# A hybrid decoder block on one core: the attention branch in seven block products, the pooling on GpSimd

## The chip, the cores and the metric

The kernel runs on one core of a Trainium2 chip. The core has TensorE (PE, matmuls; its weight loads are PEld), VectorE (DVE), ScalarE (ACT), GpSimd (POOL) and SyncE (SP, which issues DMAs); each takes its own instructions in order. The metric is the device time of one launch in microseconds (us); less is better.

## What is computed

The input x is 1024 tokens by 1024 channels, in float32. The part of the reference that the change touches:

```
xn = rmsnorm(x); u, q, k, v, gates = split(xn @ w_in + b_in)     # u: 512 wide, gates: 2 x 1024
for gi, w in enumerate((2, 4, 8, 16)):                           # four groups of 128 channels of u
    c  = cumsum(u_group over time)
    pooled = (c[t] - c[t - w]) / min(t + 1, w)                   # mean of the last w tokens
    diff[gi] = pooled - u_group
yp = einsum(diff, w_pool) * pool_scale                           # pooling branch, 512 wide
ya = sliding_window_attention(q, k, v, sinks)                    # attention branch, 512 wide
y  = sigmoid(gate0) * (yp @ w_branch_pool) + sigmoid(gate1) * (ya @ w_branch_attn)
x  = x + rmsnorm(y @ w_out)
x  = x + rmsnorm(relu(rmsnorm(x) @ w_up) ** 2 @ w_dn)
```

## The kernel before

Everything is feature-major: a tile holds 128 features in its partitions and 1024 tokens. Each float32 operand is split into two parts, hi (a rounded copy, made by ScalarE) and lo (the rest, a difference made by VectorE; both in `split`, L101 and L104), and each product is three matmul passes: hi·hi, hi·lo, lo·hi. A matmul is 128×128 weights by 512 tokens.

**Seven products for a pair of tiles.** The gate, u, out, up and down products are done for two output tiles (a pair p) and two halves of the tokens at a time, in seven products of block sums in place of eight of blocks (class `Pairs`, line 482 on). The operands of the moving side are the blocks B11, B22, B21 and the sums T1 to T4 (`OPERAND`); VectorE makes the sums of the weights of a pair (L530, L531, L535, L536), ScalarE and VectorE split them, and the seven results are summed in PSUM or by VectorE.

**The gate loop** (L1085 to L1120) runs over p = 1 to 6. A round holds five products of TensorE, 12 matmuls each: 6 of pair p, 4 and 3 of pair p−1, 5 and 7 of pair p. ScalarE copies banks out. VectorE adds product 5 into the result of pair p−1 (L1095, it reads the PSUM bank `e`; product 3 of pair p−1 goes into the same bank behind it), makes the weight sums of pair p+1, splits them, adds the third product (L1110, from PSUM) and multiplies both tiles by the norm's factor (L1105, L1112, `rb`). The gates' sigmoid follows on ScalarE and the result is stored.

**The pooling** lies in the same loop. Pairs 8 and 9 are the four tiles of u. `gate_finish` (L798) multiplies such a tile by `rb`; `chain_start` (L753) adds the bias on ScalarE and stores u to DRAM; `chain_steps` (L760) doubles a window on VectorE: t[s] = f[s] + f[s − step], an add of 128×1024 (L770) and a small copy of its first columns (L771). The four groups (windows 4, 16, 2, 8 started in p = 1, 2, 3, 4) take ten such adds in all, in p = 3 to 6 and one behind the loop. Later, while the attention product runs, u is loaded again (`pool_load`), VectorE scales and subtracts (`pool_diff`, L784 to L786) and the result is split (`pool_split`).

**The attention product** (L1146 to L1215) is done without block sums: eight output tiles m, each with 4 × 2 × 3 matmuls (`mm_fm`, L461). Its operand is four tiles of ya, split into `yahi` and `yalo` (L1055, L1060), the weights are split tile by tile (`ba_split`), and VectorE multiplies each result by its gate (`ba_mul`). The pooling branch's product follows with the same function, operand `yp`.

**Load 19** is the raw weight tile of u's last quarter; pair 9 takes it. SP issues it at the start of the gate product, behind the last stores of the attention; the sums of pair 9 (L530 at 172 us) need it. Loads of the normalised input's raw tiles `xr` follow on SP (`load_x`, L825). GpSimd issues DMAs that add into DRAM or SBUF (L438, L968) and is otherwise idle from the attention to the end.

All engines' instructions in these parts stand in the order in which the code is written (`manual_schedule`); DMAs of SP and POOL stand in their engine's order too.

Of the kernel before, what the change touches and what calls it, by code (L numbers as in the profile page):

```python
# [8 lines left out]
F32 = mybir.dt.float32  # L9
# [41 lines left out]
def block_kernel(ctx: ExitStack, tc, xt, x, consts, vecs, sinks, b_qkv, g_post, g_mlp, g_mlp_post,  # L51
# [16 lines left out]
    def nm(s):  # L68
        cnt[0] += 1
        return f"{s}_{cnt[0]}"  # L70
# [22 lines left out]
    def flat(t):  # L93
        return t.rearrange("p a b -> p (a b)")
# [657 lines left out]

    def chain_start(gi):  # L753

        f = chains[gi][0]
        act.activation(f, f, AF.Identity, bias=vec[:, V_BU + gi:V_BU + gi + 1])
        nc.sync.dma_start(u_dram[gi], f)
        chains[gi] = f, 1

    def chain_steps(gis):  # L760

        for gi in gis:
            f, step = chains[gi]
            if gi % 2 == 0:
                t = g32([S])
            elif 2 * step < WINDOWS[gi]:
                t = ga_.tile([P, S], F32, tag="ga", name=nm("t"))
            else:
                t = gate_result()
            dve.tensor_tensor(t[:, step:], f[:, step:], f[:, :S - step], ALU.add)  # L770
            dve.tensor_copy(t[:, :step], f[:, :step])  # L771
            chains[gi] = t, 2 * step

    pool_raw = {}

    def pool_load(gi):

        u = pool_raw[gi] = yy.tile([P, S], F32, tag="y", name=nm("d"))
        nc.sync.dma_start(u, u_dram[gi])

    def pool_diff(gi):

        w, (src, step), u = WINDOWS[gi], chains.pop(gi), pool_raw[gi]
        dve.scalar_tensor_tensor(u[:, w - 1:], src[:, w - 1:], 1.0 / w, u[:, w - 1:], ALU.mult, ALU.subtract)  # L784
        dve.tensor_tensor(src[:, :w - 1], src[:, :w - 1], cst[:, C_CNT:C_CNT + w - 1], ALU.mult)
        dve.tensor_tensor(u[:, :w - 1], src[:, :w - 1], u[:, :w - 1], ALU.subtract)  # L786

    def pool_split(gi):

        ysp[gi] = [flat(yp_tile([2, 512])) for _ in range(2)]  # L790
        split(*ysp[gi], pool_raw.pop(gi))
# [22 lines left out]
    def gate_result():  # L814
        return flat(yy.tile([P, 2, 512], F32, tag="y", name=nm("z")))
# [36 lines left out]
    with tc.manual_schedule(engines={mybir.EngineType.PE, mybir.EngineType.DVE, mybir.EngineType.Activation}):  # L852
# [99 lines left out]
    def g32(shape):  # L952
        return gp.tile([P] + shape, F32, tag="g", name=nm("g"))
# [23 lines left out]
    with tc.manual_schedule(engines={mybir.EngineType.PE, mybir.EngineType.DVE, mybir.EngineType.Activation,  # L977
                                     mybir.EngineType.SP}):
        gt.load(19, g32([NK, P]))
# [8 lines left out]
        for p in (6, 7):  # L988
            gt.m2(p)
            nc.sync.dma_start(f_spill(p), gt.f0.pop(p))  # L990
            if p == 6:
                gt.split37(9, ar)
                scale_gate(1)
# [52 lines left out]
    asp = [[None, None], [None, None]]  # L1046
    attn_raw = {}

    def attn_load(th, kh):
        t = attn_raw[th, kh] = xp.tile([P, 2, 512], F32R, tag="x", name=nm("yalo"))  # L1050
        nc.sync.dma_start(f32(t), y_dram[2 * kh:2 * kh + 2, :, th * 512:(th + 1) * 512].rearrange("m p q -> p m q"))

    def attn_hi(th, kh):
        hi, lo = xp.tile([P, 2, 512], F32R, tag="x", name=nm("yahi")), attn_raw[th, kh]
        act.copy(hi, f32(lo))  # L1055
        asp[th][kh] = (hi, lo)

    def attn_lo(th, kh):
        hi, lo = asp[th][kh]
        dve.tensor_tensor(lo, f32(lo), f32(hi), ALU.subtract)  # L1060

    ORDER = ((0, 0), (1, 0), (0, 1), (1, 1))

    STARTS, STEPS = {1: 1, 2: 3, 3: 0, 4: 2}, {3: (1, 1), 4: (0, 3), 5: (3, 3, 3), 6: (2, 2)}
# [4 lines left out]
    with tc.manual_schedule(engines=MANUAL):  # L1069
# [14 lines left out]
        gate_finish(17, f1s.pop(8))  # L1084
        for p in range(1, 7):  # L1085
# [5 lines left out]
            chain_steps(STEPS.get(p, ()))  # L1091
# [3 lines left out]
            dve.tensor_tensor(f1[:, V], f1[:, V], e, ALU.add)  # L1095
# [23 lines left out]
            if p in (2, 3):  # L1119
                early_third(p + 6)  # L1120

# [5 lines left out]
    def yp_tile(shape):  # L1127
        return xp.tile([P] + shape, F32R, tag="x", name=nm("yp"))

    za, ba_raw, ba_gate, ba_w, ba_bs = [], {}, {}, {}, {}  # L1130

    def ba_load(m):
        ba_gate[m] = gate_load(8 + m)
        ba_raw[m] = stage([4, P])
        nc.sync.dma_start(ba_raw[m], w_ba[m])

    def ba_split(m):
        ba_w[m] = wslot([4, P]), wslot([4, P])
        split(*ba_w[m], ba_raw.pop(m))

    def ba_mul(m):
        z = ba_gate.pop(m)
        for th, b in enumerate(ba_bs.pop(m)):
            sl = slice(th * 512, (th + 1) * 512)
            dve.tensor_tensor(z[:, sl], z[:, sl], b, ALU.mult)
        za.append(z)  # L1146

    with tc.manual_schedule(engines=MANUAL):
# [4 lines left out]
        chain_steps((2,))  # L1153
# [5 lines left out]
        attn_hi(*ORDER[0])  # L1159
        attn_lo(*ORDER[0])  # L1160
        act.copy(f1[:, U], c)
        gt.mm(e, 6, 3, after=True)
        dve.tensor_tensor(f1, f1, rb, ALU.mult)
        gate_sigmoid(13, f1)
        b7, b5 = bank("mm"), bank("at")
        gt.mm(b7, 7, 7)
        dve.tensor_tensor(f0[:, V], f0[:, V], e, ALU.add)
        ba_load(0)
        ba_load(1)
        ba_split(0)  # L1170
        attn_hi(*ORDER[1])
        dve.tensor_tensor(f0, f0, rb, ALU.mult)
        gate_sigmoid(12, f0)
        attn_hi(*ORDER[2])
        gt.mm(b5, 7, 5)
        dve.tensor_tensor(g1[:, V], u2, b7, ALU.add)
        attn_lo(*ORDER[1])
        gt.mm(b7, 7, 4, after=True)
        dve.tensor_tensor(g1[:, V], g1[:, V], b5, ALU.add)
        attn_lo(*ORDER[2])  # L1180
        attn_hi(*ORDER[3])
        ba_split(1)
        attn_lo(*ORDER[3])
        gt.mm(b5, 7, 3, after=True)
        dve.tensor_tensor(g1[:, U], u2, b7, ALU.add)
        dve.tensor_tensor(g1, g1, rb, ALU.mult)
        gate_sigmoid(15, g1)
        ba_load(2)
        POOLS = (1, 0, 3, 2)
        pool_load(POOLS[0])  # L1190
        pool_load(POOLS[1])
        for m in range(8):
            if m < 5:
                ba_load(m + 3)
            ba_bs[m] = bank("mm"), bank("mm")
            mm_fm(ba_bs[m], *ba_w[m], lambda k, hl, th: asp[th][k // 2][hl][:, k % 2, :], 4)
            if m:
                ba_mul(m - 1)
            else:
                dve.tensor_tensor(u2, u2, b5, ALU.add)  # L1200
                dve.tensor_tensor(g0, g0, rb, ALU.mult)
            if m < 6:
                ba_split(m + 2)
            if m == 0:
                gate_sigmoid(14, g0)
            if 1 < m < 6:
                pool_split(POOLS[m - 2])
            if 0 < m < 5:
                pool_diff(POOLS[m - 1])
            if 0 < m < 3:  # L1210
                pool_load(POOLS[m + 1])
# [68 lines left out]
    def bp_split(m):  # L1280
        w_of[m] = wslot([4, P]), wslot([4, P])
        split(*w_of[m], wraw_of.pop(m))
# [10 lines left out]
    with tc.manual_schedule(engines=MANUAL):  # L1293
        q1 = [wo_raw("B11", c, wraw) for c in range(2)]
        for c in range(2):
            wo_add(q1[c], "B12", c)
# [4 lines left out]
        for m in range(8):  # L1301
# [6 lines left out]
            if m:  # L1308
                bp_mul(m - 1)
            else:  # L1310
                ba_mul(7)
            if m < 7:
                bp_split(m + 1)
            if m:
                merged(m - 1)
            if m in (4, 5):
                b11[m - 4] = wo_raw("B11", m - 4, stage)
# [733 lines left out]
```

## Time and profile before

| | |
|---|---|
| median of 3 runs | 1103.01 us (1102.08 to 1103.38) |
| the profiled execution | 1100.77 us |
| its span, first to last instruction | 1098.8 us |
| granted TensorE clock | 0.998 |
| PE, DVE, ACT, POOL busy | 1088.6, 794.8, 593.8, 75.2 us |
| last attention heads and start of the gate product | 160 to 213 us |
| gate loop | 213 to 292 us |
| last gate pair | 292 to 311 us |
| attention product, then pooling product | 311 to 354, 354 to 398 us |

The table's first time is that of the launch; the profile belongs to one execution, and its span leaves out 1100.77 − 1098.8 = 2.0 us around the instructions. In rows of the trace a time of start stands first and a duration second, both in us; a bracket at the end gives the idle time of the engine ahead of the instruction and what ended it. A row of a group gives busy time and the mean in ns. A row of a DMA issue stands at the engine that issues it (SPq is SP's).

### The profile page before, as it was taken

What the parts mean: (1) busy time and instruction counts of PE and PEld (TensorE: products, weight loads), DVE (VectorE), ACT (ScalarE), POOL (GpSimd) and SP (SyncE); (2) the same over time, 40 slices, a digit from 0 to 9 for tenths busy, and PEclk for the clock granted to TensorE, in tenths of its full rate; (3) what the DMA queues carried; (4) which work ended last, traced back from release to release, by engine and by line L of the source; (5) the groups of instructions that cost most, each with busy time, mean ns of one, the idle gap of its engine ahead of it and who ended that gap; (6) DMA issues with size and microseconds to landing.
All of it is one profiled execution on the core that took longest, in us unless ns stands there. A gap on an engine that the chain in (4) does not pass through costs nothing.

```text
span 1098.8 us, 13865 instructions
## 1 busy us (share of the span) xinstructions
PE 1088.6 (99%) x5090; PEld 903.2 (82%) x5090; DVE 794.8 (72%) x1094; ACT 593.8 (54%) x976; POOL 75.2 (7%) x136
## 2 busy tenths in 40 slices
PE   9999999999999999999999999999999999999997
PEld 7888887888888888888888888888888888888886
DVE  6578897989775787979867765665557875447797
ACT  6557886455531247467655555555346535435462
POOL 0344311100000011100000000000000000000000
PEclk9999999999999999999999999999999999999999
DMA  9627889887485566932555534435697885332652
GB/s 332 169 53 190 213 235 309 250 277 278 164 283 161 168 191 127 313 101 74 184 212 211 193 139 168 148 143 193 214 385 279 292 268 188 96 96 77 222 187 90
DMA packets 93715, 216.30 MB, mean 197 GB/s; under 512 B 9936, under 2 KB 22864, under 8 KB 93648
## 3 DMA queue, kind: packets, MB, share of 16 engines
q1 hardware_dynamic: 78768, 183.04, 49.7%
q0 software_dynamic: 9408, 13.63, 7.2%
q10 hardware_dynamic: 5472, 18.75, 4.5%
q8 instruction: 40, 0.66, 0.2%
q14 instruction: 27, 0.22, 0.1%
HBM read 154.57 MB, written 59.77 MB: 195 GB/s over the span
## 4 chain that ended last, share of the span: by engine, by line
PE 92%; DMA 3%; DVE 2%; ACT 1%; issue 1%; SPq 0%; POOL 0%; DVEq 0%; ACTq 0%; POOLq 0%
PE mm L555 24%; PE at L555 18%; PE at L1819 14%; PE mm L1819 12%; PE mm L466 5%; PE mm L1354 5%; PE mm L468 3%; PE mm L183 2%; PE at L1354 2%; PE mm L192 2%; PE sc L183 2%; DMA spill_dram<-yt 1%; PE sc L428 1%; PE sc L360 1%; PE at L1400 1%
## 5 line engine op out<-in xcount | busy, mean ns | idle before, releaser
L1819 PE MATMUL at<-ar,wh 128*128 128x512 f32 x696 | 159.0, 389 | 0.2 <-DVE ar L104 0.2
L1819 PEld LDWEIGHTS at<-ar,wh 128*128 128x128 f32 x696 | 130.6, 188 | 27.7 <-DVE ar L104 0.6
L1819 PE MATMUL mm<-ar,wh 128*128 128x512 f32 x576 | 131.0, 389 | 0.0
L1819 PEld LDWEIGHTS mm<-ar,wh 128*128 128x128 f32 x576 | 108.1, 188 | 22.5
L104 DVE TENSOR_TENSOR wh<-raw,wh 128x1024 fp32r<-128x1024 f32 x50 | 61.1, 1222 | 67.5 <-ACT wh L101 67.5
L101 ACT CAST wh<-raw 128x1024 fp32r<-128x1024 f32 x50 | 52.7, 1053 | 103.2 <-PE at L1819 51.2
L101 ACT CAST wh<-st 128x512 fp32r<-128x512 f32 (+1 forms) x101 | 66.3, 662 | 62.5 <-PE mm L466 27.1
L104 DVE TENSOR_TENSOR wh<-st,wh 128x512 fp32r<-128x512 f32 (+1 forms) x102 | 75.4, 747 | 28.9 <-ACT wh L101 23.9
L555 PE MATMUL mm<-T,wx 128*128 128x512 f32 x372 | 89.5, 389 | 0.0
L555 PEld LDWEIGHTS mm<-T,wx 128*128 128x128 f32 x372 | 69.8, 188 | 14.5
L555 PE MATMUL mm<-gr,wh 128*128 128x512 f32 x321 | 77.5, 391 | 0.0
L555 PEld LDWEIGHTS mm<-gr,wh 128*128 128x128 f32 x321 | 59.8, 188 | 12.6 <-DVE gr L104 0.5
L555 PE MATMUL mm<-T,wh 128*128 128x512 f32 x267 | 66.1, 389 | 0.0
L555 PE MATMUL at<-gr,wh 128*128 128x512 f32 x243 | 59.0, 389 | 0.0
L555 PE MATMUL mm<-x,wh 128*128 128x512 f32 x240 | 58.9, 394 | 0.0
L555 PEld LDWEIGHTS mm<-T,wh 128*128 128x128 f32 x267 | 50.1, 188 | 10.4
L555 PEld LDWEIGHTS at<-gr,wh 128*128 128x128 f32 x243 | 45.6, 188 | 9.5
L104 DVE TENSOR_TENSOR ar<-B,ar 128x1024 fp32r<-128x1024 f32 x37 | 45.1, 1220 | 10.2 <-ACT ar L101 9.8
L555 PEld LDWEIGHTS mm<-x,wh 128*128 128x128 f32 x240 | 44.2, 188 | 9.6 <-ACT f L664 0.2
L555 PE MATMUL at<-T,wx 128*128 128x512 f32 x213 | 52.0, 389 | 0.0
L555 PEld LDWEIGHTS at<-T,wx 128*128 128x128 f32 x213 | 40.0, 188 | 8.3
L555 PE MATMUL at<-ar,wh 128*128 128x512 f32 x192 | 46.1, 389 | 0.0
(472 smaller groups left out, 2116.3 us busy)
## 6 DMA issues: line engine op xcount, KB each, us to landing
raw<-f_dram SPq DMA_DIRECT2D x52, 512.0 KB, 3.9
f_dram<-g SPq DMA_DIRECT2D x28, 512.0 KB, 3.1
st<-in_w_up_dram SPq DMA_DIRECT2D x24, 512.0 KB, 4.8
B<-in_w_dn_dram SPq DMA_DIRECT2D x24, 512.0 KB, 7.3
g<-spill_dram SPq DMA_DIRECT2D x19, 512.0 KB, 5.3
f_dram<-g ACTq DMA_DIRECT2D x17, 512.0 KB, 3.0
st<-in_w_g_dram SPq DMA_DIRECT2D x16, 512.0 KB, 4.9
raw<-in_w_dn_dram SPq DMA_DIRECT2D x16, 512.0 KB, 4.6
```

Of the source, the lines that this page charges most:

```text
L101: act.copy(hi, src)
L104: eng.tensor_tensor(lo, src, f32(hi), ALU.subtract)
L183: pe.matmul(bq, xs_[k][n // 4][:, xh, n % 4 * P:(n % 4 + 1) * P], wq[k][:, h, :], start=k == 0 and j == 0, stop=k == NK - 1 and j == 2)
L192: pe.matmul(bkv_of(n), xs_[k][n // 4][:, xh, n % 4 * P:(n % 4 + 1) * P], wkv[k // 2][:, h, k % 2, :], start=k == 0 and j == 0 and not (joi ...
L360: pe.matmul(sb[:, kv, i, :nk], qt[r, qx, m * P:(m + 1) * P], kx[r, k0:k0 + nk], start=j == 0, stop=j == 2)
L428: pe.matmul(yb[:, kv], v[:, c:c + P], p[ph][:, 4 * kv:4 * kv + 4].rearrange("p i q -> p (i q)"), start=j < 2, stop=j >= len(mms) - 2)
L466: pe.matmul(bs[th], whi[:, k, :], rhs(k, hl, th), start=k == 0 and hl == 0, stop=False)
L468: pe.matmul(bs[th], wlo[:, k, :], rhs(k, 0, th), start=False, stop=k == nk - 1)
L555: pe.matmul(b, w[wh][:, kt, :], x_, start=not after and kt == 0 and j == 0, stop=kt == 3 and j == 2, skip_group_check=after)
L1354: pe.matmul(bs[t], Am[a][k][ah][:, t * P:(t + 1) * P], Wm[w][k][wh], start=not after and k == 0 and j == 0, stop=k == 3 and j == 2, skip_g ...
L1400: pe.transpose(b[:, i, :], hs[4 * th + i][:, k * P:(k + 1) * P], ident)
L1819: pe.matmul(bs[t], fo[fh][:, k2, t * P:(t + 1) * P], wo_[wh][:, k2, :], start=not after and s2 == 0 and k2 == 0 and j == 0, stop=(s2, k2) ...
```

## The change

1. **Attention product in seven block products.** Four pairs of tiles; each has seven products of 2 × 3 matmuls into 512 tokens (`ba_mm`). The operands become B11, B22, B21 and T1 to T4: the four differences T are made by GpSimd in place (`attn_sum`, 128×1024 each), the weight sums by GpSimd too (`ba_sum`, four of 128×256 for a pair). Splits of the raw weights (`ba_split`, 512 and 256 wide) and of their sums (`ba_sums_hi`, `ba_sums_lo`, 1024 wide) stay on ScalarE and VectorE. The results go through three ScalarE copies and six VectorE instructions for a pair. Products 4 and 3 of the last pair stand behind the pooling product's first tile.
2. **Pooling on GpSimd.** `chain_start` adds the bias and issues all the window's adds and small copies on GpSimd; one round later `chain_end` scales by 1/w on ScalarE, multiplies the first columns by the reciprocals of their counts on GpSimd, and subtracts u on GpSimd. u stays in SBUF; its four stores and four loads are gone.
3. **Load 19** is issued in the last step of the attention, into another buffer; the split of pair 9's sums goes to other buffers (`xp_tile`).
4. `gate_finish(17)` moves from ahead of the loop to behind the first add of round 1. The first half of the out product's weight sums (`q1`) moves from ahead of the pooling product to behind its tile 1. `bp_split` takes one buffer for hi and lo.

GpSimd in the gate loop (t are the windowed sums, z_2317 and z_2360 tiles of u, f the sums of gates that a DMA adds to). Before:

```order
L968 DMA f_390_2310<-spill_dram 128x512
L968 DMA f_404_2388<-spill_dram 128x512
L968 DMA f_416_2489<-spill_dram 128x512
L968 DMA f_428_2591<-spill_dram 128x512
L968 DMA f_442_2699<-spill_dram 128x512
```

and now:

```order
L957 DMA f_404_2387<-spill_dram 128x512
L762 TENSOR_TENSOR t_2417<-z_2317 128x1023
L763 COPY t_2417<-z_2317 128x1
L762 TENSOR_TENSOR t_2420<-t_2417 128x1022
L763 COPY t_2420<-t_2417 128x2
L957 DMA f_418_2494<-spill_dram 128x512
L771 TENSOR_TENSOR t_2420<-t_2420,cst 128x3
L772 TENSOR_TENSOR z_2317<-t_2420,z_2317 128x1024
L762 TENSOR_TENSOR t_2526<-z_2360 128x1023
```

Between the DMA issues stand the adds of a window and, a round later, its difference.

VectorE in the same loop, at the turn from round 4 to round 5 (z_2828 or z_2842 the tile of pair 4). Before:

```order
L104 TENSOR_TENSOR wh_2775<-st_2702,wh_2774 128x1024
L770 TENSOR_TENSOR t_2819<-t_2709 128x1022
L771 COPY t_2819<-t_2709 128x2
L770 TENSOR_TENSOR t_2822<-t_2819 128x1020
L771 COPY t_2822<-t_2819 128x4
L770 TENSOR_TENSOR z_2825<-t_2822 128x1016
L771 COPY z_2825<-t_2822 128x8
L1095 TENSOR_TENSOR z_2828<-z_2828,at_2780 128x512
```

and now:

```order
L1111 TENSOR_TENSOR f_418_2494<-f_418_2494,rb_all 128x1024
L104 TENSOR_TENSOR wh_2798<-st_2720,wh_2797 128x1024
L1090 TENSOR_TENSOR z_2842<-z_2842,at_2803 128x512
L530 TENSOR_TENSOR ws_2857<-g_2832 128x512
L531 TENSOR_TENSOR ws_2857<-ws_2857,st_2830 128x512
```

The window's steps are gone from VectorE; the add that reads PSUM follows the last split of the round directly.

SP at the end of the attention (yt are the attention's tiles of output, xr the raw input, r_329 and g_2009 load 19):

```order
 L666 DMA spill_dram<-f_302_1832 128x1024
+L495 DMA r_329_1964<-in_w_u_dram 128x1024
+L812 DMA xr_2011<-in_xt_dram 128x1024
 L438 DMA spill_dram<-yt_1951 64x4x128 x2
 L666 DMA spill_dram<-f_318_1915 128x1024
-L692 DMA wbp_dram<-wt_1979 128x8x128
-L495 DMA g_2009<-in_w_u_dram 128x1024
-L825 DMA xr_2011<-in_xt_dram 128x1024
-L825 DMA xr_2013<-in_xt_dram 128x1024
```

Load 19 and the first load of xr now stand ahead of the last stores of yt.

The core of the diff:

```diff
     def chain_start(gi):
-        f = chains[gi][0]
+        w, f, step = WINDOWS[gi], chains[gi][0], 1
         act.activation(f, f, AF.Identity, bias=vec[:, V_BU + gi:V_BU + gi + 1])
-        nc.sync.dma_start(u_dram[gi], f)
-        chains[gi] = f, 1
-    def chain_steps(gis):
-        for gi in gis:
-            f, step = chains[gi]
...
-            dve.tensor_tensor(t[:, step:], f[:, step:], f[:, :S - step], ALU.add)
-            dve.tensor_copy(t[:, :step], f[:, :step])
-            chains[gi] = t, 2 * step
...
+        src = f
+        while step < w:
+            t = ga_.tile([P, S], F32, tag="ga", name=nm("t"))
+            pool.tensor_tensor(t[:, step:], src[:, step:], src[:, :S - step], ALU.add)
+            pool.tensor_copy(t[:, :step], src[:, :step])
+            src, step = t, 2 * step
+        chains[gi] = f, src
+    def chain_end(gi):
+        w, (f, t) = WINDOWS[gi], chains.pop(gi)
+        act.activation(t[:, w - 1:], t[:, w - 1:], AF.Identity, scale=1.0 / w)
+        pool.tensor_tensor(t[:, :w - 1], t[:, :w - 1], cst[:, C_CNT:C_CNT + w - 1], ALU.mult)
+        pool.tensor_tensor(f, t, f, ALU.subtract)
+        pool_raw[gi] = f
...
+            if n == NT - 1:
+                gt.load(19, ga_.tile([P, NK, P], F32, tag="ga", name=nm("r19")))
...
-        gt.load(19, g32([NK, P]))
...
+    def attn_sum(dst, a, b):
+        d, a, b = (flat(attn_raw[o]) for o in (dst, a, b))
+        pool.tensor_tensor(d, a, b, ALU.subtract)
...
-        gate_finish(17, f1s.pop(8))
         for p in range(1, 7):
...
-            chain_steps(STEPS.get(p, ()))
...
             dve.tensor_tensor(f1[:, V], f1[:, V], e, ALU.add)
+            if p == 1:
+                gate_finish(17, f1s.pop(8))
...
             act.copy(gt.f0[p][:, V], c)
+            if p - 1 in STARTS:
+                chain_end(STARTS[p - 1])
             if p in STARTS:
                 chain_start(STARTS[p])
...
+            if p == 6:
+                attn_block("B11", (0, 0), yp_tile)
+                attn_sum((0, 0), (1, 0), (0, 0))
+                attn_sum((1, 0), (1, 1), (1, 0))
...
+    def ba_sum(p):
+        t, q = ba_raw[p], stage([NK, P])
...
+        pool.tensor_tensor(s1, a21, a22, ALU.add)
+        pool.tensor_tensor(s2, s1, a11, ALU.subtract)
+        pool.tensor_tensor(s3, a12, s2, ALU.subtract)
+        pool.tensor_tensor(s4, a11, a21, ALU.subtract)
...
+    def ba_mm(b, p, i, after=False):
+        w, xo = ba_w.pop((p, i)), attn[OPERAND[i]]
+        for kt in range(2):
+            for j, (wh, xh) in enumerate(PASSES):
+                pe.matmul(b, w[wh][:, kt, :], xo[xh][:, kt, :], start=not after and kt == 0 and j == 0,
+                          stop=kt == 1 and j == 2, skip_group_check=after)
...
-        for m in range(8):
...
-            mm_fm(ba_bs[m], *ba_w[m], lambda k, hl, th: asp[th][k // 2][hl][:, k % 2, :], 4)
...
+        for p in range(4):
+            if p:
+                ba_m1(p)
...
+                ba_m4(p - 1)
...
+            ba_m2(p)
+            if p:
+                ba_m3(p - 1)
...
+            ba_m6(p)
...
+            ba_m5(p)
...
+            ba_m7(p)
```

More of the change, by code (lines that the diff above doesn't have):

```diff
@@ L751, in block_kernel, with pool_split @@
     chains = {}
+    pool_raw = {}
     def chain_start(gi):
[L755 removed]
+        w, f, step = WINDOWS[gi], chains[gi][0], 1
         act.activation(f, f, AF.Identity, bias=vec[:, V_BU + gi:V_BU + gi + 1])
[L757 to L790 removed]
+        src = f
[11 more added lines that the diff above has]
+        pool_raw[gi] = f
+    def pool_split(gi, tile_):
+        ysp[gi] = [flat(tile_([2, 512])) for _ in range(2)]
         split(*ysp[gi], pool_raw.pop(gi))
@@ L1044, in early_third, with attn_hi, attn_lo, attn_block @@
         gate_close(2 * p, gt.f0.pop(p))
-    asp = [[None, None], [None, None]]
-    attn_raw = {}
+    attn_raw, attn = {}, {}
     def attn_load(th, kh):
[L1050 to L1064, printed above, removed]
+        t = attn_raw[th, kh] = xp.tile([P, 2, 512], F32, tag="x", name=nm("ya"))
+        nc.sync.dma_start(t, y_dram[2 * kh:2 * kh + 2, :, th * 512:(th + 1) * 512].rearrange("m p q -> p m q"))
+    def attn_hi(name, o, tile_):
+        attn[name] = hi, _ = tile_([2, 512]), tile_([2, 512])
+        act.copy(flat(hi), flat(attn_raw[o]))
+    def attn_lo(name, o):
+        hi, lo = attn[name]
+        dve.tensor_tensor(flat(lo), flat(attn_raw[o]), flat(f32(hi)), ALU.subtract)
+    def attn_block(name, o, tile_):
+        attn_hi(name, o, tile_)
+        attn_lo(name, o)
+    def attn_sum(dst, a, b):
+        d, a, b = (flat(attn_raw[o]) for o in (dst, a, b))
+        pool.tensor_tensor(d, a, b, ALU.subtract)
+    ORDER = ((0, 0), (1, 0), (1, 1), (0, 1))
+    def yp_tile(shape):
+        return xp.tile([P] + shape, F32R, tag="x", name=nm("yp"))
+    STARTS = {1: 1, 2: 3, 3: 0, 4: 2}
     ysp = {}
@@ L1125, in gate_load @@
         return t
[L1127 to L1146, printed above, removed]
+    za, ba_raw, ba_sums, ba_w, ba_z = [], {}, {}, {}, {}
@@ new lines, in ba_put, with ba_split, ba_sums_hi @@
+    def ba_put(p, items, hi, lo):
+        for j, i in enumerate(items):
+            ba_w[p, i] = tuple(t[:, 2 * j:2 * j + 2] for t in (hi, lo))
+    def ba_split(p):
+        for a, b, items in ((0, 4, (1, 2)), (4, 6, (4,))):
+            t = wslot([2, b - a, P])
+            split(flat(t[:, 0]), flat(t[:, 1]), flat(ba_raw[p][:, a:b]))
+            ba_put(p, items, t[:, 0], t[:, 1])
+    def ba_sums_hi(p):
+        hi = wslot([NK, P])
+        act.copy(flat(hi), flat(ba_sums[p]))
+        ba_sums[p] = ba_sums[p], hi
@@ new lines, in ba_m1, with ba_m2, ba_m6, ba_m5 @@
+    def ba_m1(p):
+        ba_first[p], ba_chain[p] = bank("at"), bank("mm")
+        ba_mm(ba_first[p], p, 1)
+        act.copy(ba_chain[p], ba_first[p])
+    def ba_m2(p):
+        b, z = ba_first.pop(p), ba_z[p][0]
+        ba_mm(b, p, 2, after=True)
+        dve.tensor_tensor(z[:, U], z[:, U], b, ALU.mult)
+    def ba_m6(p):
+        ba_f[p] = ga_.tile([P, S], F32, tag="ga", name=nm("fv"))
+        ba_mm(ba_chain[p], p, 6, after=True)
+        act.copy(ba_f[p][:, U], ba_chain[p])
+    def ba_m5(p):
+        ba_fifth[p] = bank("at")
+        ba_mm(ba_fifth[p], p, 5)
@@ new lines, in ba_m7, with ba_m4, ba_m3 @@
+    def ba_m7(p):
+        f, z = ba_f[p][:, V], ba_z[p][1]
+        ba_mm(ba_chain[p], p, 7, after=True)
+        act.copy(f, ba_chain[p])
+        dve.tensor_tensor(f, f, ba_fifth[p], ALU.add)
+        dve.tensor_tensor(z[:, V], z[:, V], f, ALU.mult)
+    def ba_m4(p):
+        b, z = ba_chain.pop(p), ba_z[p][1]
+        ba_mm(b, p, 4, after=True)
+        dve.tensor_tensor(z[:, U], z[:, U], b, ALU.mult)
+    def ba_m3(p):
+        b, z, f = ba_fifth.pop(p), ba_z[p][0], ba_f.pop(p)[:, U]
+        ba_mm(b, p, 3, after=True)
+        dve.tensor_tensor(f, f, b, ALU.add)
+        dve.tensor_tensor(z[:, V], z[:, V], f, ALU.mult)
@@ L1152, in block_kernel @@
         gt.mm(b6, 7, 6)
-        chain_steps((2,))
+        ba_load(0)
+        ba_load(1)
+        ba_sum(0)
         act.copy(f1[:, V], c)
@@ L1315, in block_kernel @@
                 merged(m - 1)
+            if m == 1:
+                q1 = [wo_raw("B11", c, wraw) for c in range(2)]
+                for c in range(2):
+                    wo_add(q1[c], "B12", c)
             if m in (4, 5):
```

104 lines of the change are left out of this document (63 added, 41 removed).

## The prediction

> **What bounds the kernel now.** I read the share of each engine first, then what TensorE waits for, then the chain of work that ended last, then the engines' busy time in the stretches that the change touches.
>
> ```profile
> PE 1088.6 (99%) x5090; PEld 903.2 (82%) x5090; DVE 794.8 (72%) x1094; ACT 593.8 (54%) x976; POOL 75.2 (7%) x136
> ```
>
> ```profile
> PE mm L201 <- DVE pad L160: 1.1, 1, 1.1
> PE at L555 <- DVE ar L104: 0.5, 1, 0.5
> PE at L555 <- ACT ar L101: 0.3, 1, 0.3
> ```
>
> TensorE is busy for 1088.6 of 1098.8 us, and its longest wait is 1.1 us. So a matmul taken away is time taken away, but only while the other engines keep up. Who has room shows by stage: the gate loop (210.5 to 292.1), one round of it, and the start of the attention product. Behind each stretch and its length stand PE, PEld, DVE, ACT and POOL busy, the clock, the DMA share and GB/s.
>
> ```profile
> 210.50:292.10 81.60, 81.60 (x362) 67.57 (x361) 75.60 (x96) 45.70 (x57) 2.65 (x3) 1.00 0.74 244
> 292.10:311.00 18.90, 18.90 (x86) 15.63 (x85) 12.85 (x16) 9.04 (x11) 0.00 (x0) 1.00 0.57 194
> 248.00:262.00 14.00, 14.00 (x63) 11.62 (x62) 13.61 (x19) 8.16 (x11) 0.00 (x0) 1.00 0.81 287
> ```
>
> In the loop VectorE is the second bound: 13.61 of 14 us in that round. GpSimd does nothing there but a few DMA issues, and the change gives it the pooling.
>
> **Matmuls taken away: −5.4.** The attention product has 64 matmuls in each of three passes; two are on L466, one on L468.
>
> ```profile
> L466 PE MATMUL mm<-yahi,wh x64: 389/389/390, 311.0 to 353.6; 128*128 128x512 f32 x64
> L466 PE MATMUL mm<-yalo,wh x64: 389/389/390, 311.2 to 353.8; 128*128 128x512 f32 x64
> ```
>
> ```profile
> 398.19 21.76 PE mm L1354 x96
> 270.35 5.44 PE at L555 x24
> ```
>
> 192 become 4 pairs of tiles × 7 products × 2 × 3 = 168. They are pipelined, so the price is that of a run of them in the chain: 21.76 / 96 = 0.2267 us. 24 × 0.2267 = 5.44. The last two products now stand behind the pooling product's first tile, which covers their sums; I charge nothing there.
>
> **Load 19 moved: +1.0 (−0.9 to +4.3).** SP issues it ahead of the loads of xr now.
>
> ```profile
> 176.21 0.73 PE L555 MATMUL at<-x,ar 128*128 128x512 f32 x2 [0.34 <-ACT ar L101]
> 177.47 2.56 PE L555 MATMUL at<-x,ar 128*128 128x512 f32 x10 [0.53 <-DVE ar L104]
> 196.75 1.52 PE L555 MATMUL mm<-gr,wh 128*128 128x512 f32 x6
> ```
>
> ```profile
> 172.28 0.69 DVE L530 TENSOR_TENSOR ws<-g 128x512 f32<-128x512 f32 x1 [3.24 <-DMA g<-in_w_u_dram]
> 194.08 2.43 DVE L104 TENSOR_TENSOR gr<-xr,gr 128x1024 fp32r<-128x1024 f32 x2
> ```
>
> ```profile
> 161.56 1.25 SPq L438 DMA_DIRECT2D spill_dram<-yt  x2
> 164.86 1.79 SPq L495 DMA_DIRECT2D g<-in_w_u_dram  x1
> 168.40 0.81 SPq L825 DMA_DIRECT2D xr<-in_xt_dram  x2
> 182.37 0.81 SPq L825 DMA_DIRECT2D xr<-in_xt_dram  x2
> ```
>
> VectorE waited 3.24 us for this load, and behind it TensorE 0.34 + 0.53; the load in front takes both away (−0.87). Against it: the first xr load waits for a buffer until 168.4, and the last store of yt (161.56 before) now stands behind it on SP. GpSimd's sum of that tile, and the xr load at 182.37 that waits for it, follow up to 6 us later. That load feeds the split at 194.08, whose result TensorE uses at 196.75, and TensorE does not wait there now. The conversion had under 2 us of slack, so 0 to 4.3 us comes through. I take 1.9 of it less 0.87, near the low end because the first 2 us of the delay meet the transfer's spare time.
>
> **Pooling on GpSimd in the gate loop: +12.5 (0 to +18).** What the diff seems to do is free VectorE. What the trace shows is that the two engines hold each other up. VectorE's rows, then GpSimd's:
>
> ```profile
> 82.77 0.79 DVE L104 TENSOR_TENSOR wh<-st,wh 128x512 fp32r<-128x512 f32 x1
> 83.48 0.74 DVE L283 SCALAR_TENSOR_TENSOR tf<-mm,r,bc 128x512 f32<-128x512 f32 x1
> 97.29 1.30 DVE L677 SCALAR_TENSOR_TENSOR wh<-st,vec,wh 128x1024 fp32r<-128x1024 f32 x1
> 98.51 0.94 DVE L104 TENSOR_TENSOR wh<-st,wh 128x512 fp32r<-128x512 f32 x1
> ```
>
> ```profile
> 82.73 0.29 POOL L103 CAST v<-vf 128x128 fp32r<-128x128 f32 x1
> 83.10 0.78 POOL L104 TENSOR_TENSOR v<-vf,v 128x128 fp32r<-128x128 f32 x1
> 84.34 0.46 POOL L104 TENSOR_TENSOR dv<-df,dv 128x128 fp32r<-128x128 f32 x1
> 97.58 1.33 POOL L104 TENSOR_TENSOR v<-vf,v 128x128 fp32r<-128x128 f32 x1
> ```
>
> GpSimd's 128x128 difference takes 0.46 alone (84.34), 0.78 where it meets VectorE, 1.33 where it meets the 128x1024 instruction of 97.29: in both it ends 0.32 after VectorE's instruction (83.56, 98.59). The other way, the sum at 98.51 takes 0.94, 0.25 over its usual 0.69, and the one at 82.77 ends 0.53 after GpSimd's cast (83.02). L283 reads PSUM and takes its 0.74 beside GpSimd unhurt. So a VectorE instruction with both inputs in SBUF and a GpSimd instruction take turns. The rows show that for waits up to 1 us; I take it to hold for the whole length of the new instructions.
>
> [...]
>
> GpSimd's price for 128x1024 comes from two sizes:
>
> ```profile
> L297 POOL TENSOR_TENSOR qkv<-qkv,cst 128x160 f32<-128x160 f32 x4 | 2.1, 532 | 13.6 <-DVE qkv L286 9.6 <-ACT khi L101 4.0
> L299 POOL TENSOR_TENSOR qkv<-qkv,rb 128x80 f32<-128x80 f32 x4 | 1.4, 356 | 0.0
> ```
>
> (532 − 356) / 80 = 2.2 ns an element and 0.18 us fixed: 2.43 us, of which 2.25 streams. A VectorE instruction of that size takes 1.22 (213.12, 264.43 below). [...]
>
> ```profile
> 213.12 1.22 DVE L800 TENSOR_TENSOR z<-z,rb_all 128x1024 f32<-128x1024 f32 x1
> 250.76 0.68 DVE L1043 TENSOR_TENSOR g<-g,g 128x512 f32<-128x512 f32 x1
> 255.02 0.68 DVE L1095 TENSOR_TENSOR z<-z,at 128x512 f32<-128x512 f32 x1
> 264.43 1.22 DVE L770 TENSOR_TENSOR t<-t 128x1022 f32<-128x1022 f32 x1
> 268.30 0.68 DVE L1095 TENSOR_TENSOR z<-z,at 128x512 f32<-128x512 f32 x1
> ```
>
> A round of VectorE without pooling and gates lasts from 255.02 to 264.43, 9.41 us. From 213.12 to the add of round p = 5 (before: L1095 at 268.30, 1.4 us ahead of the product that starts at 270.35 in its bank) there are four such rounds, 37.6, and the gates of p = 1 to 3, four instructions of 1.22 and two of 0.68 to 0.69: 6.3. Together 43.9. GpSimd has ten adds and three differences in the same time, 13 × 2.25 = 29.3, and 13 small instructions of about 0.1, 1.3. Sum 74.5. Two VectorE adds a round read PSUM and may run beside GpSimd: 8 × 0.68 = 5.4 off. 69.1 us behind 213.12 is 282.2; with the add itself 282.9 against 270.35: 12.5 late. The start of each product in that bank waits for this add, so TensorE shows it all. Laid out instruction by instruction in turn it comes to 13.2; without anything beside, 18; with GpSimd's adds slipping into later rounds, which have 4 us of room each, 8; without exclusion, 0, since VectorE alone needs 43.9 of 57.2.
>
> ScalarE scales by 1/w once GpSimd is through, and its queue (8.16 of 14 us busy) is held behind; I charge nothing, since the same rounds already wait for VectorE.
>
> **Start of the attention product: +2.4 (0 to +4).** Before, VectorE had 12.85 of 18.9 us there (row above), up to the product's first matmul. Its four splits of 128x1024 become nine up to the use of T4 (operands and weight sums): 12.85 + 5 × 1.22 = 19.0, and two more small weight splits make it about 20. GpSimd has four differences of 2.43 and eight 128x256 sums of 0.74 (0.18 + 256 × 2.2 ns): 15.6. Less 4.8 (seven adds of 0.69 that read PSUM and run beside), 31 us; TensorE has 120 matmuls, 27.2 us, in that stretch. 3.8 late at most, of which gaps take some.
>
> **Costs at nothing.** The DMAs of u (four stores, four loads) leave SP, which nothing waits for here. The sum for the out product moves behind pooling tile 1; its cast follows tens of microseconds later. The z gate of tile 17 moves behind the first add of the loop, which helps that add by 1.2 us; counted above.
>
> **The sum.** −5.4 + 1.0 + 12.5 + 2.4 = +10.5. The profiled execution took 1100.77 us, so 1111.3 by it; the median of the runs is 1103.01, 2.2 above, so 1113.5 there, which I give.
>
> **Rivals.**
>
> *The long GpSimd instructions hinder nothing* (or VectorE wins every turn, and GpSimd's backlog is never waited for). Then VectorE has 13 us more room in the loop, 43.9 of 57.2, the start of the attention product has only 20 of 27.2, and the sum is −5.4 − 0.9: 1103.0 − 6.3 = 1096.7. For it: no row shows a hold by GpSimd of over 0.6 us. Against it: the rows that exist fit taking turns to 0.03 us. It decides at 57.2 − 43.9 = 13.3: if less than that of GpSimd's 30.6 us in the loop excludes VectorE, the loop ends in time. 22%.
>
> *Half the price*: GpSimd holds only a part of each instruction, or its work lags into rounds with room. Half of the late time, (12.5 + 2.4) / 2 = 7.5, gives −5.4 + 1.0 + 7.5 = +3: 1106. The bounds of load 19 carry it from 1103 to 1109. 23%.
>
> *No overlap at all*: PSUM adds wait too, because VectorE is in order and stands behind a blocked one: loop 18, start 4, sum +17.6: 1120.6. 8%.
>
> **How the numbers follow.** The forecast, 1113.5 with 1108.5 (loop 8) to 1118 by its own terms, gets 47%. A measurement of this kernel tells about 0.2%, 2.2 us, from no change. Faster by more than that: the first rival and a small part of the second, 23%. Within: the lower end of the second, 6%. Slower: 71%. The range goes from 1096 to 1119 and leaves out the last rival and tails.
>
> **What would show it.** Right: in the loop TensorE idle behind VectorE's add at L1090, together 8 to 15 us from p = 2 to p = 5; VectorE 1024-sums of 2.5 to 3.5 us where 1.22 stood, adds of 0.68 from PSUM unchanged; GpSimd adds over 2.43. The attention product's own 168 matmuls 38.1 us. Wrong: VectorE's sums stay at 1.22 beside GpSimd's adds, or TensorE's waits in the loop stay under 2 us, or a wait near 190 of more than 5 us carries the loss.

## The result and the profile after

| | before | after |
|---|---|---|
| median | 1102.55 us (4 runs, 1100.98 to 1103.38) | 1115.36 us (4 runs, 1114.18 to 1118.33) |
| profiled execution, its span | 1100.77, 1098.8 | 1114.18, 1112.4 |

The ratio is 1.0122, with a 95% interval of 1.0098 to 1.0146: slower by 1.2%; the forecast was 1113.5, slower by 1.0%. First the share of the engines, the longest waits of TensorE, and the loop's stretch (PE, PEld, DVE, ACT, POOL busy, clock, DMA share, GB/s):

```profile
PE 1088.5 (98%) x5066; PEld 901.2 (81%) x5066; DVE 820.8 (74%) x1077; ACT 608.9 (55%) x999; POOL 150.7 (14%) x184
```

```profile
PE mm L555 <- ACT z L1089: 10.2, 3, 6.0
PE at L555 <- ACT wx L101: 2.5, 1, 2.5
PE mm L201 <- DVE pad L160: 1.1, 1, 1.1
PE at L1908 <- DVE hold L104: 0.8, 1, 0.8
PE mm L1178 <- DVE yp L1046: 0.7, 1, 0.7
```

```profile
210.50:300.00 89.50, 79.33 (x339) 64.52 (x338) 84.60 (x75) 46.30 (x58) 48.82 (x32) 0.96 0.61 193
```

TensorE has 24 matmuls less and yet is as long busy. In the loop it stands for 10 of 89.5 us, its clock is at 0.96 there, and GpSimd is busy for 48.8 us where it was for 2.7.

**A ledger of the stages.** ScalarE's copies that follow a product at once are marks that both kernels have: the first and the sixth copy `f<-mm` of the loop (rounds 1 and 6) and TensorE's first matmul of the out product. Before, then after:

```profile
213.32 0.59 ACT L1099 COPY f<-mm 128x512 f32<-128x512 f32 x1 [2.19 <-PE mm L555]
281.27 0.59 ACT L1099 COPY f<-mm 128x512 f32<-128x512 f32 x1 [2.13 <-PE mm L555]
...
398.03 0.39 PE L1354 MATMUL mm<-B11h,gr 128*128 128x512 f32 x1
```

```profile
216.44 0.59 ACT L1096 COPY f<-mm 128x512 f32<-128x512 f32 x1 [2.19 <-PE mm L555]
297.36 0.59 ACT L1096 COPY f<-mm 128x512 f32<-128x512 f32 x1 [1.59 <-PE mm L555]
...
411.08 0.39 PE L1443 MATMUL mm<-B11h,gr 128*128 128x512 f32 x1
```

Up to round 1 the kernel is 3.12 us late. The five rounds take 80.92 us and not 67.95: +12.97. From round 6 to the out product it takes 113.72 and not 116.76: −3.04, which with the 5.44 us of matmuls taken away is a loss of 2.40. Behind that +0.55. Sum 13.6, the difference of the spans. The forecast had +1.0, +12.5, −5.4 + 2.4, and nothing behind.

**The loop: one engine shuts the other out.** GpSimd's rows of round 1 and one of round 2, then VectorE's beside them:

```profile
219.20 1.89 POOL L762 TENSOR_TENSOR t<-z 128x1023 f32<-128x1023 f32 x1 [7.04 <-ACT z L758]
221.04 0.63 POOL L763 COPY t<-z 128x1 f32<-128x1 f32 x1
221.76 2.23 POOL L762 TENSOR_TENSOR t<-t 128x1022 f32<-128x1022 f32 x1
...
244.91 2.66 POOL L762 TENSOR_TENSOR t<-t 128x1016 f32<-128x1016 f32 x1
```

```profile
219.29 2.35 DVE L535 TENSOR_TENSOR st<-st,ws 128x512 f32<-128x512 f32 x1
221.56 0.68 DVE L536 TENSOR_TENSOR st<-st,r 128x512 f32<-128x512 f32 x1
222.16 2.91 DVE L104 TENSOR_TENSOR wx<-ws,wx 128x1024 fp32r<-128x1024 f32 x1
...
245.31 0.67 DVE L1109 TENSOR_TENSOR f<-f,at 128x512 f32<-128x512 f32 x1
```

The sum L535 takes 0.69 otherwise; here it ends at 221.64, 0.55 behind GpSimd's add (221.09). The split takes 1.22 otherwise, and ends 1.08 behind the second add (223.99). The other way, GpSimd's copy of a single column takes 0.63: it stands behind L535 and ends with it (221.67). L1109 reads PSUM and takes its usual 0.67 in the middle of GpSimd's add of 244.91.

**How that reaches TensorE.** ScalarE's rows in round 3, then TensorE's:

```profile
248.69 1.15 ACT L794 ACTIVATE f<-f,vec 128x1024 f32<-128x1024 f32 x1 [1.28 <-DVE f L1111]
249.87 0.33 ACTq L795 DMA_DIRECT2D spill_dram<-f  x1
250.30 0.58 ACT L1089 COPY z<-mm 128x512 f32<-128x512 f32 x1 [0.46 <-ACT f L794]
```

```profile
250.94 1.65 PE L555 MATMUL mm<-T,wh 128*128 128x512 f32 x3 [5.98 <-ACT z L1089]
252.38 3.42 PE L555 MATMUL mm<-gr,wh 128*128 128x512 f32 x9
```

VectorE's late multiply (L1111) holds ScalarE's sigmoid, behind it in ScalarE's order stands the copy of the bank (L1089), and TensorE's product 4 waits 5.98 us for that copy. Then its matmuls run slowly: 3.42 us for nine, against 2.20 in other rounds. The stretches show the granted clock, third from the end:

```profile
248.00:252.00 4.00, 1.06 (x3) 0.88 (x4) 3.96 (x5) 2.85 (x4) 2.28 (x3) 0.51 0.55 124
252.00:256.00 4.00, 4.00 (x13) 3.17 (x12) 3.93 (x4) 1.66 (x3) 2.64 (x1) 0.64 0.81 276
```

**The start of the attention product.** One of GpSimd's differences, VectorE's weight splits beside it, and the part of TensorE's first product that uses them:

```profile
322.39 2.41 POOL L1054 TENSOR_TENSOR ya<-ya,ya 128x1024 f32<-128x1024 f32 x1 [2.95 <-issue]
```

```profile
322.76 2.92 DVE L104 TENSOR_TENSOR wh<-st,wh 128x512 fp32r<-128x512 f32 x2 [0.51 <-ACT wh L101]
```

```profile
325.40 1.19 PE L1178 MATMUL at<-yp,wh 128*128 128x512 f32 x4 [0.43 <-DVE wh L104]
```

The two splits take 1.02 together where GpSimd is idle (at 332.60); here they take 2.92, and TensorE waits 0.43 us for the first of them. Its other wait of the stretch, 0.7 us (L1178 in the list above), is for the lo part of T3, which VectorE makes.

**Load 19.** The rows of SP, of VectorE and of TensorE:

```profile
156.01 0.42 SPq L495 DMA_DIRECT2D r<-in_w_u_dram  x1
168.38 0.33 SPq L812 DMA_DIRECT2D xr<-in_xt_dram  x1
168.80 1.25 SPq L438 DMA_DIRECT2D spill_dram<-yt  x2
170.09 0.62 SPq L666 DMA_DIRECT2D spill_dram<-f  x1
```

```profile
174.43 0.69 DVE L530 TENSOR_TENSOR ws<-r 128x512 f32<-128x512 f32 x1 [5.50 <-DMA spill_dram<-f]
```

```profile
178.31 0.73 PE L555 MATMUL at<-x,wx 128*128 128x512 f32 x2 [2.55 <-ACT wx L101]
179.56 4.14 PE L555 MATMUL at<-x,wx 128*128 128x512 f32 x10 [0.52 <-DVE wx L104]
```

The load itself is early (156.01), but SP then stands still until 168.38 for the first xr's buffer (11.7 us, until a store of yt has landed). The store of f behind it is at 170.09, not 162.90 as before, and L530's buffer waits for that store. TensorE waits 2.55 + 0.52, and again its next ten matmuls run slowly (4.14 us).

### The profile page after: what moved, and what is told of

Read it like the earlier page. It is cut to its first block, busy times and chain, and to the rows that moved or that the text cites. A ratio compares the mean times of both kernels' runs of the same rounds, so it can differ in the third digit from the quotient of the medians.

```text
span 1112.4 us, 13876 instructions
## 1 busy us (share of the span) xinstructions
PE 1088.5 (98%) x5066; PEld 901.2 (81%) x5066; DVE 820.8 (74%) x1077; ACT 608.9 (55%) x999; POOL 150.7 (14%) x184
## 4 chain that ended last, share of the span: by engine, by line
PE 82%; DVE 9%; DMA 3%; issue 3%; ACT 2%; SPq 0%; POOL 0%; ACTq 0%; DVEq 0%; POOLq 0%
PE mm L555 20%; PE at L555 15%; PE at L1908 12%; PE mm L1908 11%; PE mm L1443 5%; PE mm L466 3%; PE mm L192 2%; PE sc L183 2%; PE mm L183 2%; PE at L1443 2%; PE at L1178 2%; PE mm L1178 1%; PE mm L468 1%; DMA g<-in_w_g_dram 1%; DVE wh L104 1%
## 5 line engine op out<-in xcount | busy, mean ns | idle before, releaser
L104 DVE TENSOR_TENSOR wh<-st,wh 128x512 fp32r<-128x512 f32 (+2 forms) x102 | 75.9, 754 | 26.1 <-ACT wh L101 21.7
L555 PE MATMUL mm<-T,wh 128*128 128x512 f32 x267 | 67.1, 393 | 10.2 <-ACT z L1089 10.2
```

The lines of the kernel that those rows point to most:

```text
L104: eng.tensor_tensor(lo, src, f32(hi), ALU.subtract)
L555: pe.matmul(b, w[wh][:, kt, :], x_, start=not after and kt == 0 and j == 0, stop=kt == 3 and j == 2, skip_group_check=after)
```

## The experiments

The marks of the ledger for each kernel, as differences from the first profile of before (us): up to round 1; the five rounds; from round 6 to the out product, which holds the −5.44 of the matmuls where the seven products are in; the span. Median and ratio are against before on the same chip.

| | to round 1 | rounds 1 to 6 | to out product | span | median (before) | ratio, 95% |
|---|---|---|---|---|---|---|
| after | +3.12 | +12.97 | −3.04 | +13.6 | 1115.36 (1102.55) | 1.0122 (1.0098 to 1.0146) |
| e1 | −0.28 | +11.58 | −3.03 | +8.3 | 1110.28 (1101.40) | 1.0085 (1.0063 to 1.0107) |
| e2 | +3.43 | +7.76 | −2.95 | +7.8 | 1108.84 (1101.40) | 1.0067 (1.0052 to 1.0082) |
| e3 | +2.81 | 0 | 0 | +3.1 | 1104.62 (1101.40) | 1.0033 (1.0020 to 1.0046) |
| e4 | +2.52 | +26.92 | −0.92 | +29.4 | 1130.65 (1101.40) | 1.0270 (1.0250 to 1.0289) |
| e5 | +3.11 | 0 | −3.05 | +0.5 | 1101.10, one run (1102.01) | – |
| e6 | +0.31 | −0.01 | +1.81 | +2.4 | 1104.75 (1102.01) | 1.0025 (1.0014 to 1.0036) |
| e7 | −1.29 | 0 | +3.44 | +2.6 | 1102.50 (1102.01) | 1.0006 (0.9998 to 1.0015) |
| e8 | −1.86 | +0.02 | +2.15 | +0.5 | 1101.19 (1102.01) | 0.9992 (0.9984 to 1.0001) |
| e9 | −1.45 | 0 | +5.18 | +4.5 | 1103.75 (1102.00) | 1.0014 (1.0002 to 1.0026) |
| e10 | −2.18 | −0.01 | +6.14 | +4.4 | 1107.04 (1102.00) | 1.0052 (1.0034 to 1.0069) |
| e11 | −1.46 | −0.01 | −2.20 | −4.0 | 1098.51 (1101.75) | 0.9972 (0.9961 to 0.9983) |

**e1: load 19 back** (from the changed kernel).

```diff
-            if n == NT - 1:
-                gt.load(19, ga_.tile([P, NK, P], F32, tag="ga", name=nm("r19")))
...
+        gt.load(19, g32([NK, P]))
         load_x(1, lambda: flat(yy.tile([P, 2, 512], F32, tag="y", name=nm("xr"))))
```

> The changed kernel with load 19 issued where it was before, so that SP's first xr load stands behind the last stores of yt and f again. Theory (SP stands still behind the xr load; the store of f behind it is late, and VectorE's sums of pair 9 wait for that store's buffer): the gate stage is 3.1 us shorter, 1112.2 us (1111 to 1113.5), and VectorE's first L530 at 172 instead of 174.4. Rival (the early load gains 0.9 us, and the 3.1 us come from the other buffers or from elsewhere): 1115.4 to 1116.3. The loop's loss stays at about 13 us in both.

The 3.1 us of the gate stage are gone (3.40 between the marks of after and e1), and VectorE's first L530 is at 172.07. On a chip where before takes 1.15 us less, 1110.28 lies in the theory's range. The loop's loss was 1.4 us smaller in this profile than in after's; why, no run here tells.

**e2: the pooling's instructions on VectorE**, at the same places of the code.

```diff
-            pool.tensor_tensor(t[:, step:], src[:, step:], src[:, :S - step], ALU.add)
-            pool.tensor_copy(t[:, :step], src[:, :step])
+            dve.tensor_tensor(t[:, step:], src[:, step:], src[:, :S - step], ALU.add)
+            dve.tensor_copy(t[:, :step], src[:, :step])
```

and the same for `chain_end`'s two.

> The changed kernel with the window adds, the small copies and the differences of chain_start and chain_end issued on VectorE instead of GpSimd, at the same places of the code. Theory (GpSimd's 128x1024 instructions and VectorE's shut each other out): VectorE then has 43.9 + 10 x 1.3 + 3 x 1.2 = 60.5 us of work in 57.2, the loop loses about 3 to 5 us instead of 13, so 1106 us (1103 to 1109). Rival (the loss comes from the windows' place in the order, one round after another, with ScalarE waiting for their end, and not from the engine): the loop keeps 8 us or more of its loss, 1110 to 1116.

The same work on the engine that was full already costs 5.2 us less than on the idle one. But the loop still loses 7.76, more than the 3 to 5 expected and just under the rival's 8. TensorE's three waits add up to 5.3 us; the slow stretch after the longest, 3.23 us (twelve matmuls in 4.45 us), was in no sum of mine.

**e3: load 19 alone** (from the kernel before).

```diff
+            if n == NT - 1:
+                gt.load(19, ga_.tile([P, NK, P], F32, tag="ga", name=nm("r19")))
...
-        gt.load(19, g32([NK, P]))
...
-                gt.split37(9, ar)
+                gt.split37(9, xp_tile)
```

> The kernel before with load 19 moved into the last step of the attention alone (and the split of pair 9 into the other buffers). Theory (SP stands still behind the xr load): 3.1 us more than before, 1105.7 us (1104.5 to 1107). Rival (the early load takes VectorE's wait of 3.24 us and TensorE's 0.87 away): 1101.7.

+2.81 at the mark, +3.2 in the median: the theory. The load moved alone has the same cost and no other.

**e4: each window add twice** (from the changed kernel).

```diff
             pool.tensor_tensor(t[:, step:], src[:, step:], src[:, :S - step], ALU.add)
+            pool.tensor_tensor(t[:, step:], src[:, step:], src[:, :S - step], ALU.add)
```

> The changed kernel with each of GpSimd's ten window adds issued twice (the second writes the same again). Theory (turns with VectorE): ten more holds of 2.25 us, less a few that fall into VectorE's gaps: 15 to 23 us more, 1131 to 1138 us. Rival (no exclusion; VectorE is late for another reason): GpSimd is idle for 40 us of the loop's 89.5 and takes the 24 us there, 0 to 5 us more, 1115 to 1120.

Ten more adds, 13.95 us more in the loop, though GpSimd had been idle for 33 of the 81 us (47.96 busy between the marks of after). In the whole span it is 15.8 us more, the low end of the theory's 15 to 23. The rival is out. A row of this run also gives the price of an add alone, for VectorE is idle for the 3.54 us ahead of 299.04:

```profile
296.99 1.89 POOL L763 TENSOR_TENSOR t<-t 128x1020 f32<-128x1020 f32 x1
```

```profile
299.04 0.69 DVE L530 TENSOR_TENSOR ws<-g 128x512 f32<-128x512 f32 x1 [3.54 <-POOL t L764]
```

So the ten added adds are 18.9 us of work and not 22.5, and 74% of it comes through in the loop.

**e5: memsets instead of window adds** (the windows' sums are left out).

```diff
-            pool.tensor_tensor(t[:, step:], src[:, step:], src[:, :S - step], ALU.add)
-            pool.tensor_copy(t[:, :step], src[:, :step])
+            pool.memset(t, 0.0)
+            pool.memset(t, 0.0)
```

> The changed kernel with each window add of GpSimd and its small copy replaced by two memsets of the same 128x1024 tile: the windows' sums are left out, GpSimd stays about as long busy in the same places, but it only writes SBUF there. Theory (what shuts VectorE out is GpSimd reading SBUF while VectorE reads two operands there): VectorE's sums beside the memsets keep their 0.69 and 1.22 us, only the three differences hold it up, and the loop loses 0 to 4 us instead of 13: about 1103 us (1101 to 1106). Rival 1 (any GpSimd work in SBUF shuts VectorE out): loss as before, 1112 to 1115. Rival 2 (the order of the code, with ScalarE waiting for GpSimd): also 1110 or more, but with VectorE's sums at 0.69 and 1.22.

GpSimd is busy for 30.2 us of the five rounds here, for 48.0 in after, its own waits for VectorE included. GpSimd's rows, then VectorE's beside them:

```profile
236.95 0.95 POOL L763 MEMSET t<- 128x1024 f32 x1
237.84 0.96 POOL L762 MEMSET t<- 128x1024 f32 x1
238.86 0.97 POOL L763 MEMSET t<- 128x1024 f32 x1
```

```profile
236.22 0.68 DVE L104 TENSOR_TENSOR wh<-r,wh 128x512 fp32r<-128x512 f32 x1
236.83 0.67 DVE L1109 TENSOR_TENSOR f<-f,at 128x512 f32<-128x512 f32 x1
237.53 1.23 DVE L1111 TENSOR_TENSOR f<-f,rb_all 128x1024 f32<-128x1024 f32 x1
238.98 1.23 DVE L104 TENSOR_TENSOR wh<-st,wh 128x1024 fp32r<-128x1024 f32 x1 [0.22 <-ACT wh L101]
```

Nothing is held up beside the memsets. The differences, which GpSimd still makes and which read SBUF, do hold VectorE in the same execution:

```profile
272.45 2.39 POOL L772 TENSOR_TENSOR g<-t,g 128x1024 f32<-128x1024 f32 x1 [4.99 <-ACT t L770]
```

```profile
273.28 2.65 DVE L104 TENSOR_TENSOR wx<-ws,wx 128x1024 fp32r<-128x1024 f32 x1 [1.26 <-ACT wx L101]
```

VectorE has room for these, and the rounds take 67.95 us to the hundredth, those of before. So it is neither GpSimd's being busy nor the order of the code with `chain_end`, which is unchanged; it is GpSimd reading SBUF while VectorE reads two operands there: VectorE's 128×1024 instructions keep their 1.23 us beside the memsets, which only write SBUF, and one takes 2.65 beside the difference. (A memset doesn't wait for the bias as an add does and starts earlier, so this says nothing of a wait there: those of the first window are through at 216.84, and the first add of after starts at 219.20.)

**e6 to e8: the seven products without the pooling's move.** e6 has the pooling of before (VectorE, u through DRAM) and load 19 where it was. e7 has the early load, and the first xr load in a buffer of the later pool. e8 is e7 with all block sums on VectorE. The edits of e7 and e8:

```diff
-        load_x(1, lambda: flat(yy.tile([P, 2, 512], F32, tag="y", name=nm("xr"))))
+        load_x(1, g_place)
...
-        pool.tensor_tensor(d, a, b, ALU.subtract)
+        dve.tensor_tensor(d, a, b, ALU.subtract)
...
-        pool.tensor_tensor(s1, a21, a22, ALU.add)
+        dve.tensor_tensor(s1, a21, a22, ALU.add)
```

> The seven products alone: pooling on VectorE with u through DRAM and load 19 where it was, both as in the kernel before. Theory (the pooling on GpSimd costs the 13 us of the loop, the load 3): the matmuls' -5.4, the attention's start +2.4, and up to 3 us because two operand sums now lie beside VectorE's window adds in round 6: 1098.4 to 1101.4 where before is 1101.4, ratio 0.997 to 1.000. Rival (the seven products themselves cost as much as they save, in VectorE's and ScalarE's extra splits): 1102 or more.

> As the seven products alone, and load 19 issued early as in the change, but with the first xr load going to a buffer of the later pool, so that it stands behind the last stores on SP. Theory (the early load is good for 0.87 us of TensorE's wait if SP does not stand still): 0.9 us less than the seven products alone, VectorE's first L530 of pair 9 before 171. Rival (the load's own ga buffer makes VectorE's sums wait): 0 to 3 us more.

> The kernel of seven products with the early load, and with all block sums of the attention product (four of 128x1024, sixteen of 128x256) on VectorE instead of GpSimd. Theory (a GpSimd sum costs VectorE its whole 2.4 or 0.74 us, a VectorE sum 1.14 or 0.4): VectorE's load up to T4 falls from 31 to about 25 us in 27.2, the attention's start loses nothing: 1.5 to 3 us less than with the sums on GpSimd. Rival (GpSimd works beside VectorE in the gaps, so VectorE is later with the sums on it): 1 to 3 us more.

e6 went to its rival: 1.81 us more up to the out product, so 7.25 lost where the matmuls bring 5.44. The likely reason is that the pooling's differences, back on VectorE, now stand there; TensorE's waits in that stretch are mostly for VectorE's splits. e7: the load gives 1.60 us against e6 once SP does not stand still (L530 at 169.67 instead of 172.65), more than the 0.87 that I had seen in TensorE's waits. But e7's profile loses 1.63 us more than e6's from round 6 to the out product, where the code of the two is the same; a difference of that size in this column is not safe by itself. e8: 1.29 us less than e7 in that column, and 1.3 in the median, just under the range expected. The medians, of 11 runs each, bear it out: sums on the full engine are a little cheaper than on the idle one here too.

**e9 to e11: where the differences stand.** e9 is e7 with `attn_sum` on VectorE, and each difference just ahead of its split; e10 is e9 with `attn_sum` on GpSimd; e11 is e9 with each difference at the end of the pair before, in place of the calls at the splits:

```diff
             ba_m7(p)
+            if p < 3:
+                pool_diff(POOLS[p])
+            if p < 2:
+                pool_load(POOLS[p + 2])
+            if p == 2:
+                pool_diff(POOLS[3])
```

> The kernel of seven products with the early load, its four operand sums of 128x1024 on VectorE, the weight sums on GpSimd, and the pooling's differences made just ahead of their splits, from the second pair on. Theory (the start of the attention product is bound by VectorE and what shuts it out, up to the last split of T4): 19.0 + 4 x 1.14 + small = 25 us against 27.2 there, so it loses 0 to 3 us instead of 9, and the gate stage gains 1.3: 1.3 + 5.4 less 1.5 = 5 us less than before, ratio 0.994 to 0.998. Rival (ScalarE's order or the differences' place further on hold the product just as much): ratio 0.999 or more.

> The same with the four operand sums on GpSimd. Theory (turns with VectorE): 19.0 + 4 x 2.4 + the part of the weight sums that meets VectorE, 31 us against 27.2, 2 to 4 us more than with the sums on VectorE, ratio 0.997 to 1.001. Rival (GpSimd's sums lie in VectorE's gaps): no more than the other.

> As the kernel with the operand sums on VectorE and the weight sums on GpSimd, but with each of the pooling's differences made at the end of the pair before its split, so that ScalarE's cast of it does not wait (4.1 us of TensorE's waits stood behind ScalarE's copies of fv, 2.4 behind the last split of yp). Theory (these waits were the differences' place, and VectorE has room otherwise): the waits of 2.3, 1.75, 1.6 and 0.8 us go, 4 to 7 us less than with the differences at the split, ratio to before 0.994 to 0.998. Rival (VectorE is full in that stretch, whatever the order): 0.999 or more, with VectorE's weight splits waited for instead.

e9 went to its rival, and its rows say why: TensorE's waits, then ScalarE's rows at the first of them.

```profile
PE mm L1190 <- ACT fv L1206: 4.1, 2, 2.3
PE mm L466 <- ACT yp L101: 1.6, 1, 1.6
```

```profile
326.76 1.04 ACT L101 CAST yp<-d 128x1024 fp32r<-128x1024 f32 x1 [5.28 <-DVE d L786]
327.72 0.58 ACT L1206 COPY fv<-mm 128x512 f32<-128x512 f32 x1
```

ScalarE waits 5.28 us for the difference, and the copy of a bank stands behind it. e10 is 3.3 us above e9 in the median, as expected of turns, but the spans of the two profiles are alike (4.4 and 4.5), so what makes it is not shown. e11 moves a few calls and takes 7.38 us from e9's stage and 5.2 from its median, as the theory had it; TensorE's waits there are down to 1.8 us, now for VectorE's weight splits. It is faster than both kernels: 0.9972 (0.9961 to 0.9983) of before.

## Why the prediction was right, step by step

- **The loop, +12.5: measured 12.97, by the mechanism named.** Turns between GpSimd and VectorE hold for GpSimd's instructions of 1.9 to 2.8 us (after's rows, e4, e5) as for its cast of 0.29 in before; the forecast had taken that over from rows of up to 1.33 us. Three things were not as written. TensorE did not wait for VectorE's add L1090 but one product earlier, for ScalarE's copy L1089 behind a sigmoid. I had charged ScalarE's order at nothing "since the same rounds already wait for VectorE": it is the same wait, seen through another engine, though it comes from the sigmoids and not from the scaling by 1/w. GpSimd's price was too high: a window add takes 1.89 alone (e4's row) and not 2.43, and of the ten adds of after only three take more than 2.43, which was to be a sign. With ten at 1.89 and three differences at 2.40 in place of 13 × 2.25 the sum falls by about 3.2, to 9.3; that is an estimate from these rows. The 0.1 us of each small instruction was an estimate that no row gave; e4's copy at 298.82 takes 0.19 alone, which would bring back about 1.2. And the waits are 10.2 us, not 12.5; TensorE's slow matmuls, in no sum of mine, make most of the other 2.8. So the near-exact figure is partly luck: one price too high, one cost left out.
- **Matmuls −5.44 and the start of the product +2.4: measured −3.04 together, forecast −3.0.** e5 and e2 have the same −3.05 and −2.95, so it doesn't hang on the loop. The mechanism shows in after's rows at 322: a GpSimd difference holds a split for which TensorE waits. How much of the 2.40 such turns make no run here tells.
- **Load 19, +1.0: measured 3.12, inside its bounds.** This term was mis-sized. The path that I charged +1.9 for, from the store of yt to the split at 194, cost nothing: the xr load comes 3.85 us later (186.22), and TensorE does not wait there. The step that failed is "the load in front takes both away (−0.87)": VectorE's wait of 3.24 did not go but grew to 5.50, for another cause, the store of f behind the xr load on SP. I had followed the store of yt past SP's stop and not the store of f, which is in the same queue. e1 and e3 show the term alone, e7 what the load is worth with SP free.
- **The rivals.** No hindrance (1096.7) fell with after's rows and e4. That the memsets of e5, which hinder nothing, leave 1101.1 and not 1096.7 is the load's 3.1, in place of −0.9, and the start's 2.4 still in it. Half the price fell with the loop's 12.97; its lower end should have been 1104 and not 1103 (1106 less 1.9). No overlap at all fell with the adds that read PSUM, which keep their 0.67 beside GpSimd.

## What to carry to other kernels

An idle engine is not a free one (the loop took 5.2 us more with the pooling on GpSimd than with it on the full VectorE, e2): before work is moved to GpSimd, look at what VectorE does at that moment, and count most of GpSimd's SBUF-reading time as VectorE's where VectorE is full and reads two operands from SBUF (74% in e4). Of a DMA that is issued earlier, follow everything that it is moved past in its queue, stores included, to the buffers that wait for them (3.12 us here). In an engine's fixed order a late operand costs what stands behind the instruction that needs it (in e9 5.28 us of ScalarE's and 4.1 us of TensorE's, in two waits); moving the producer forward a little (5.2 us in the median, e11) can be worth more than a faster engine (1.3, e7 to e8).

## What the hardware showed that I had not expected

A wait of TensorE can cost more than itself. After the wait of 5.98 us its clock was 0.51 and 0.64 in the two stretches shown above, and the 120 matmuls from 250.94 on took 29.4 us instead of 27.2. After 2.55 and 0.52 us with two matmuls between, ten matmuls took 4.14 us instead of 2.56. A wait of 3.12 us in the same execution left the clock at full:

```profile
280.00:284.00 4.00, 0.88 (x5) 0.49 (x4) 2.88 (x3) 2.99 (x5) 2.27 (x3) 1.00 1.01 385
284.00:288.00 4.00, 4.00 (x19) 3.32 (x18) 3.93 (x4) 3.36 (x5) 2.72 (x1) 1.00 0.71 258
```

A wait's length alone does not tell which of the two follows. With two matmuls between, the waits of 2.55 and 0.52 us in after went with a clock of 0.60 from 180 to 184. In e2, behind a single wait of 3.23 us, little more than the 3.12 above, twelve matmuls took 4.45 us (247.62 to 252.07), where twelve took 2.86 behind its wait of 1.80 us (278.52 to 281.38). What decides it is left open: no run was made for it.
